# A hybrid encoder step: the second mixer's projections gathered ahead of its blocks, 13 unit pairs by seven products

## The chip, the cores and the metric

One core of a Trainium2 chip. The metric is the device time of one execution in microseconds (us), given as the median of several runs. TensorE is called PE in the rows of the profile (PEld where it loads weights), VectorE DVE, ScalarE ACT, GpSimd POOL; SP issues most of the DMAs.

## The reference

Two layers over 640 tokens (512 of a prompt, and 8 streams of 16): an FFN, a mixer and an FFN in each, each with a layer norm. The change lies in the second layer's mixer:

```python
proj = x @ w_in                       # 640 x 1024 by 1024 x (2048 gates z, 3072 xbc, 32 dt)
ext = concatenate([conv_state, xbc])  # three older rows ahead of each stream
xbc = silu(conv_b + sum(ext[:, w:w + length] * conv_w[w] for w in range(4)))
xs, bm, cm = ...                      # 4 groups of 8 heads; state of 128
dt = softplus(dt_raw + dt_bias)
y, h_last = ssd_recurrence(xs, dt, a, bm, cm, h0)   # chunk by chunk: causal part, then the carried state
yg = (y + d_skip * xs) * silu(z)
out = (yg * rsqrt(mean(square(yg)) + eps) * norm_g) @ w_out
```

## The kernel before

Every fp32 operand of the large matmuls is split into two fp32r parts, hi (a copy on ACT) and lo (the rest, a subtraction on DVE, line 101), and a product is hi·hi + hi·lo + lo·hi. x stands in SBUF as `xhi` and `xlo`, 8 blocks of 128 channels by 640 tokens. Weights come from memory into `raw` (four buffers of 128x1024) and are split into `w` (six buffers; `w1` holds one half-size unit).

A *unit* is 128 columns of an input projection. The plain way (`load_w`, `cm_proj`, `mm3`, line 146) takes it in two halves of 256 and 384 tokens, 24 matmuls each. The FFNs' gate and up projections work instead on *pairs* of units by seven products (`operands`, `matrix`, `product`, line 366): the weights of the pair and x are taken as 2x2 blocks, sums of blocks are formed (four of weights for each pair, on DVE, line 349; T1, T2, T4 and a fourth sum of x once), seven products of 12 matmuls over 320 tokens are made, and results are kept back on ACT (line 379) and added again.

The second mixer has 4 groups. A group has 6 xbc units (its B, C and four x units) and 4 gate units. `xbc` projects a unit into a row `ext` beside older rows, then convolves: the first step on ACT (1576), three taps on DVE (1578), Tanh on ACT (1580), two closing steps on DVE (1583, 1585); the result is stored in `bcx_d`. `gate_in` projects a gate unit and stores it in `z_d`. POOL fills `ext`'s older rows and copies the last rows out (1549 to 1570). A group is worked through in five *blocks* of 128 tokens: the streams (c = 4, `core_s`) first, then the prompt's four chunks in sequence (`core_b`); `core_a` prepares a block (loads of `bx`, `csb`, `ecs`; decays on DVE and ACT; small matmuls 1691 to 1701). `gate_out` gates a finished block, norms it and projects it out into `yacc` (24 matmuls of 512 columns, line 146 on `og`).

The order: four half units, dt and group 0's units come first; then 20 steps, one block each, with group g+1's xbc units and group g's gates as *fill* (`fill`, `run_fill`), up to two units a step. `gate_out` follows a group later. Within what buffers and dependencies allow, a scheduler places each engine's instructions, as the order below shows them.

Of the kernel before, what the change touches and what calls it, by code (L numbers as in the profile page):

```python
# [37 lines left out]
def kernel(ctx: ExitStack, tc: tile.TileContext, I, O, phases=PHASES):  # L38
# [186 lines left out]

    def ffn(i, ph, last, side=None):
# [3 lines left out]
        Q = T // 2  # L230
        with ExitStack() as st:
# [73 lines left out]
            hf32, lf32 = xh.bitcast(F32), xl.bitcast(F32)  # L305
            quad = lambda t, a, b: t[:, 4 * a:4 * a + 4, Q * b:Q * b + Q]

            tq = {n: wk.tile([128, 2, 4, Q], F32R, name=f"T{n}", bufs=1) for n in (1, 2, 4)}

            def both(t, p, m, op):  # L310

                u = wk.tile([128, T], F32, name="hf", bufs=2)[:, :Q]
                V.tensor_tensor(t, quad(hf32, *p)[:, k], quad(hf32, *m)[:, k], op=op)
                V.tensor_tensor(u, quad(lf32, *p)[:, k], quad(lf32, *m)[:, k], op=op)
                V.tensor_tensor(t, t, u, op=ALU.add)

            t2, t3 = (wk.tile([128, 4, Q], F32, name="h", bufs=4) for _ in range(2))
            for k in range(4):
                t1 = wk.tile([128, Q], F32, name="mx", bufs=2)
                both(t1, (0, 1), (1, 1), ALU.add)  # L320
                both(t3[:, k], (0, 0), (0, 1), ALU.subtract)
                for part in (hf32, lf32):
                    V.tensor_tensor(t2[:, k], t1 if part is hf32 else t2[:, k], quad(part, 0, 0)[:, k], op=ALU.subtract)
                split(tq[1][:, 0, k], tq[1][:, 1, k], t1)
                split(tq[2][:, 0, k], tq[2][:, 1, k], t2[:, k])

# [4 lines left out]
            for k in range(4):  # L331
                V.tensor_tensor(t2[:, k], quad(hf32, 1, 0)[:, k], t2[:, k], op=ALU.subtract)
                V.tensor_tensor(t2[:, k], t2[:, k], quad(lf32, 1, 0)[:, k], op=ALU.add)
                split(tq[4][:, 0, k], tq[4][:, 1, k], t2[:, k])
            X = {1: (quad(xh, 0, 0), quad(xl, 0, 0)), 2: (quad(xh, 1, 0), quad(xl, 1, 0)),
                 4: (quad(xh, 1, 1), quad(xl, 1, 1)), 3: (tq[4][:, 0], tq[4][:, 1]), 5: (tq[1][:, 0], tq[1][:, 1]),
                 6: (tq[2][:, 0], tq[2][:, 1]), 7: (quad(xh, 0, 1), quad(xl, 0, 1))}

            def operands(src0, src1):
                r0, r1 = raw_tile(), raw_tile()  # L340
                nc.sync.dma_start(r0, src0)
                nc.sync.dma_start(r1, src1)
                b11, b21, b12, b22 = r0[:, :512], r0[:, 512:], r1[:, :512], r1[:, 512:]
                u, v, w = (two_units() for _ in range(3))
                o = unit()

                def total(o, v, w):
                    with tc.issue_after(state["lo"]):
                        V.tensor_tensor(o, v, w, op=ALU.subtract)  # L349

                split2(u, r0)
                state["lo"] = split(v[:, 1, 0], v[:, 1, 1], b22).ins
                total(b11, b12, b11)
                split(v[:, 0, 0], v[:, 0, 1], b11)
                total(b12, b22, b12)
                total(b22, b22, b11)
                split2(w, r1)
                total(b21, b21, b22)
                split(o[:, 0], o[:, 1], b21)
                return {1: u[:, 0], 2: u[:, 1], 3: v[:, 1], 4: o, 5: v[:, 0], 6: w[:, 1], 7: w[:, 0]}  # L360

            def product(ps, A, p, first):
                n = 0
                for a, b in ((0, 0), (0, 1), (1, 0)):
                    for k in range(4):
                        nc.tensor.matmul(ps, A[p][:, a, k * 128:k * 128 + 128], X[p][b][:, k, :],  # L366
                                         start=(first and n == 0), stop=(n == 11), skip_group_check=True)
                        n += 1

            def matrix(A, take):  # L370

                z = sums[0]
                sums.reverse()
                x, w = (bank("a")[:, :Q] for _ in range(2))
                e = {}

                def keep(n, ps):
                    e[n] = wk.tile([128, Q], F32, name="mx", bufs=2)
                    nc.scalar.copy(e[n], ps)  # L379


                product(x, A, 1, True)
                nc.scalar.copy(z, x)  # L383
                product(w, A, 5, True)
                keep(5, w)
                product(z, A, 6, False)
                keep(2, z)
                product(x, A, 2, False)
                take(0, 0, x, None)
                product(z, A, 7, False)  # L390
                take(1, 1, z, e[5])
                product(w, A, 3, False)
                take(1, 0, w, e[2])
                product(z, A, 4, False)
                take(0, 1, z, None)
# [4 lines left out]
            def pair(f, before=None):  # L400
# [25 lines left out]
                for n, take in (("w_gate", gate), ("w_up", up)):  # L426
# [14 lines left out]
                    matrix(A, take)  # L441
# [1055 lines left out]
    def mixer1(ph, last):  # L1497
# [6 lines left out]
        with ExitStack() as st:  # L1504
            wk = pool("m1", 1, st, reuse_waits="tile")
            def after_norm():

                q = ExitStack()
                for n in ("pow", "ln"):
                    if n in state:  # L1510
                        q.enter_context(tc.issue_after(state[n]))
                return q

            with after_norm():
# [10 lines left out]
                cvo = {}  # L1525
# [12 lines left out]
            def row_tile(n):  # L1538
                return wk.tile([128, 667], F32, name=n, bufs=2)


            xin = {}

            def xbc_half(g, u, h):
                if h == 0:
                    m = (16 + g, 20 + g)[u] if u < 2 else 4 * g + u - 2
                    ext = row_tile("ext")
                    xin[g, u] = load_w(I["m1_in"][10 * g + u]), ext, m
                    G.memset(ext[:, 0:3], 0.0)
                    es_ = ext[:, 515:667].rearrange("p (b i) -> p b i", i=19)  # L1550
                    G.tensor_copy(es_[:, :, 0:3], cst[:, m].rearrange("p (b i) -> p b i", i=3))
                wt, ext, _ = xin[g, u]
                es_ = ext[:, 515:667].rearrange("p (b i) -> p b i", i=19)
                o, L = HALVES[h]
                ps = cm_proj(wt, h)
                if h == 0:
                    nc.scalar.copy(ext[:, 3:3 + L], ps[:, :L])
                else:
                    nc.scalar.copy(ext[:, 3 + o:515], ps[:, :512 - o])
                    nc.scalar.copy(es_[:, :, 3:19], ps[:, 512 - o:L].rearrange("p (b i) -> p b i", i=16))  # L1560

            def xbc(g, u):
                for h in range(0 if (g, u) not in xin else 1, 2):
                    xbc_half(g, u, h)
                _, ext, m = xin[g, u]
                es_ = ext[:, 515:667].rearrange("p (b i) -> p b i", i=19)
                if u == 0:
                    cvo[g] = wk.tile([128, 6, 27], F32, name="cvo", bufs=1)
                G.tensor_copy(cvo[g][:, u, 0:3], ext[:, 512:515])
                G.tensor_copy(cvo[g][:, u, 3:27].rearrange("p (b i) -> p b i", i=3), es_[:, :, 16:19])  # L1570
                if u == 5:
                    nc.sync.dma_start(O["conv"][:, 6 * g:6 * g + 6], cvo[g])
# [4 lines left out]
                for w in range(1, 4):  # L1577
                    V.scalar_tensor_tensor(acc[:, :n], ext[:, w:w + n], cw[:, m, w:w + 1], acc[:, :n],
                                           op0=ALU.mult, op1=ALU.add)
                nc.scalar.activation(ext[:, :n], acc[:, :n], AF.Tanh)  # L1580
                runs = lambda t: t[:, 515:667].rearrange("p (b i) -> p b i", i=19)[:, :, :16]
# [19 lines left out]
            def gate_in(g, q):  # L1601

                for h in range(0 if (g, q) not in zin else 1, 2):
                    gate_half(g, q, h)
                nc.sync.dma_start(z_d[g][:, :, q, :], zin[g, q][1].rearrange("p (c t) -> p c t", t=128))
# [7 lines left out]
            dt, cs = (wk.tile([32, T], F32, name=n) for n in ("dt", "cs"))  # L1613
            rst, te = (wk.tile([128, 1024], F32, name="csb", bufs=2)[:32, :T] for _ in range(2))
# [43 lines left out]
            def core_a(g, c):  # L1658
                bx = wk.tile([128, 6, 128], F32, name="bx", bufs=2)
# [4 lines left out]
                csb = wk.tile([128, 1024], F32, name="csb", bufs=2).rearrange("p (h t) -> p h t", t=128)  # L1664
# [6 lines left out]
                else:  # L1671
                    e8 = wk.tile([128, 8, 8], F32, name="e8")
# [4 lines left out]
                if 0 < c < 4:  # L1677
                    ecs = wk.tile([128, 4, 128], F32, name="ecs", bufs=1)
# [5 lines left out]
                elif c == 4:  # L1684
                    ecs = wk.tile([128, 8], F32, name="ecs8")
# [7 lines left out]
                cbm = wk.tile([128, 128], F32, name="cbm", bufs=2)  # L1693
# [3 lines left out]
                bk = wk.tile([128, 128], F32, name="bk", bufs=2)  # L1697
# [122 lines left out]
            for u in range(1, 6):  # L1820
                if u == 2:
                    gate_in(0, 0)
                    dt_rest()
# [196 lines left out]
```

## Time and profile before

| | |
|---|---|
| median of 3 runs | 2525.39 us (2525.12 to 2529.2) |
| the profiled execution | 2531.27 us, its span 2529.6 us |
| busy: TensorE, VectorE, ScalarE, GpSimd | 98%, 80%, 50%, 15% |
| second mixer in the span | about 1587 to 2084 us |

In a row of the instructions in order of time stand start, duration, engine, line, operation, output and inputs, shapes and count; in square brackets how long the engine had been idle and what ended that. A row of groups has the count, then the busy time, the mean in ns, and idle time before it. Rows of stretches give each engine's busy time between two moments. A matmul's duration includes its way through the pipeline; what one costs in a row of many is the distance of the starts.

### The profile page before, as it was taken

To read this page: it belongs to the slowest core of one execution; us is meant where nothing else is said; L and a number is where in the kernel's file an instruction comes from. 1 tells how busy PE (TensorE), PEld (TensorE's weight loads), DVE (VectorE), ACT (ScalarE), POOL (GpSimd) and SP (SyncE) were. 2 spreads that over 40 slices of the span, in tenths; PEclk is the share of its full clock that TensorE was granted. 3 is DMA by queue.
4 is the path that set the end of the run, shared out by engine and by line. 5 is a ranking of instruction groups with operands and counts; after the bars stand their busy time and mean duration, and the time that the engine had idled before them with its cause. 6 is when DMAs were issued, how large, how long until landed. Compare 5 with 4: busy or idle time off the path is not lost. (4 is left out here: it accounts for less than half of the span.)

```text
span 2529.6 us, 40802 instructions
## 1 busy us (share of the span) xinstructions
PE 2490.1 (98%) x15551; PEld 2286.1 (90%) x15551; DVE 2014.5 (80%) x3505; ACT 1269.2 (50%) x2389; POOL 373.5 (15%) x492
## 2 busy tenths in 40 slices
PE   9999999999999999999999999999999999999998
PEld 8999999878789999999999999998999879999897
DVE  7788777676879888877988887787575789998887
ACT  4444344336744555553555554566465543554542
POOL 0000001210130000013000002311121152111121
PEclk9999999999999999999999999999999999999999
DMA  5332335443222433452144434556464723555563
GB/s 186 109 100 78 116 112 161 144 150 117 87 79 64 119 102 97 112 164 66 59 114 113 120 100 132 158 162 204 137 211 137 242 74 99 154 151 165 151 172 116
DMA packets 179253, 324.80 MB, mean 128 GB/s; under 512 B 21312, under 2 KB 92608, under 8 KB 178544
## 3 DMA queue, kind: packets, MB, share of 16 engines
q1 hardware_dynamic: 165200, 293.83, 36.9%
q0 software_dynamic: 13856, 28.35, 5.8%
q8 instruction: 122, 2.00, 0.3%
q14 instruction: 75, 0.61, 0.1%
HBM read 259.56 MB, written 40.54 MB: 119 GB/s over the span
## 5 line engine op out<-in xcount | busy, mean ns | idle before, releaser
L100 ACT CAST w<-raw 128x512 fp32r<-128x512 f32 (+1 forms) x721 | 532.7, 769 | 337.3 <-DVE raw L349 144.7
L101 DVE TENSOR_TENSOR w<-raw,w 128x512 fp32r<-128x512 f32 (+2 forms) x721 | 621.2, 883 | 86.9 <-ACT w L100 84.0
L366 PE MATMUL bank<-xhi,w 128*128 128x320 f32 x2432 | 436.2, 309 | 2.3 <-DVE s L408 1.4
L366 PE MATMUL bank<-T,w 128*128 128x320 f32 x2736 | 428.2, 310 | 5.3 <-ACT bank L383 2.7
L366 PEld LDWEIGHTS bank<-T,w 128*128 128x128 f32 x2736 | 406.8, 188 | 8.6 <-ACT bank L383 5.3
L366 PEld LDWEIGHTS bank<-xhi,w 128*128 128x128 f32 x2432 | 376.8, 188 | 6.6 <-DVE s L408 2.2
L146 PE MATMUL bank<-xhi,w 128*128 128x256 f32 (+2 forms) x2272 | 364.3, 312 | 5.2 <-ACT xhi L100 2.6
L146 PEld LDWEIGHTS bank<-xhi,w 128*128 128x128 f32 x2272 | 337.3, 189 | 15.8 <-issue 4.9
L146 PE MATMUL bank<-w,h 128*128 128x512 f32 x1488 | 346.5, 391 | 0.2 <-DVE yacc L223 0.2
L146 PEld LDWEIGHTS bank<-w,h 128*128 128x128 f32 x1488 | 277.2, 188 | 57.9 <-ACT h L100 1.6
L366 PE MATMUL bank<-xlo,w 128*128 128x320 f32 x1216 | 227.8, 309 | 0.0
L349 DVE TENSOR_TENSOR raw<-raw 128x512 f32<-128x512 f32 x304 | 214.0, 704 | 3.4
L366 PEld LDWEIGHTS bank<-xlo,w 128*128 128x128 f32 x1216 | 190.8, 188 | 0.0
L146 PE MATMUL bank<-xlo,w 128*128 128x256 f32 (+2 forms) x1136 | 190.0, 309 | 0.0
L515 POOL DMA_DIRECT2D yacc<-ev x84 | 72.6, 893 | 690.2 <-ACT ev L514 619.8
L146 PEld LDWEIGHTS bank<-xlo,w 128*128 128x128 f32 x1136 | 171.6, 188 | 0.6
L502 PE MATMUL bank<-w,h 128*128 128x512 f32 x576 | 134.5, 390 | 0.0
L502 PEld LDWEIGHTS bank<-w,h 128*128 128x128 f32 x576 | 107.9, 188 | 22.7 <-DVE yacc L511 0.2
L379 ACT COPY mx<-bank 128x320 f32<-128x320 f32 x152 | 64.6, 425 | 105.9 <-PE bank L366 105.2
L223 DVE SCALAR_TENSOR_TENSOR yacc<-bank,yacc 128x512 f32<-128x512 f32 x120 | 82.0, 687 | 40.3 <-PE bank L146 39.7
L511 DVE SCALAR_TENSOR_TENSOR yacc<-bank,yacc 128x512 f32<-128x512 f32 x84 | 57.8, 688 | 67.4 <-PE bank L502 67.4
L146 PE MATMUL bank<-w,og 128*128 128x512 f32 x432 | 103.1, 394 | 0.0
(437 smaller groups left out, 3359.0 us busy)
## 6 DMA issues: line engine op xcount, KB each, us to landing
raw<-in_w_gate_dram SPq DMA_DIRECT2D x88, 512.0 KB, 3.7
raw<-in_w_up_dram SPq DMA_DIRECT2D x88, 512.0 KB, 3.8
raw<-in_w_down_dram SPq DMA_DIRECT2D x88, 512.0 KB, 3.6
raw<-in_m_in_dram SPq DMA_DIRECT2D x52, 512.0 KB, 4.6
yacc<-ev POOLq DMA_DIRECT2D x84, 256.0 KB, 4.7
raw<-in_m_out_dram SPq DMA_DIRECT2D x24, 512.0 KB, 4.3
csb<-cs_d SPq DMA_DIRECT2D x20, 512.0 KB, 5.3
h<-in_ssd_h_dram SPq DMA_DIRECT2D x16, 512.0 KB, 6.6
```

What stands on the lines that cost most here:

```text
L100: nc.scalar.copy(hi, src)
L101: return nc.vector.tensor_tensor(lo, src, hi.bitcast(F32), op=ALU.subtract)
L146: state["pe"] = nc.tensor.matmul(ps, a, b, start=(k == 0), stop=(k == n - 1)).ins
L223: state["acc"] = nc.vector.scalar_tensor_tensor(ya, pb, scale, ya, op0=ALU.mult, op1=ALU.add).ins
L349: V.tensor_tensor(o, v, w, op=ALU.subtract)
L366: nc.tensor.matmul(ps, A[p][:, a, k * 128:k * 128 + 128], X[p][b][:, k, :], start=(first and n == 0), stop=(n == 11), skip_group_check=True)
L379: nc.scalar.copy(e[n], ps)
L502: nc.tensor.matmul(ps, a[:, u], b[:, v], start=(first and n == 0), stop=(n == 5), skip_group_check=True)
L511: V.scalar_tensor_tensor(ya, ps, 0.5 / ALPHA, ya, op0=ALU.mult, op1=ALU.add)
L515: nc.gpsimd.dma_start(yacc[:, t, 512 * j:512 * j + 512], e, accum_op=ALU.add)
```

## The change

The FFNs keep their seven products; `x_sums`, `seven_x`, `operands` and `matrix` become functions that the second mixer calls too. The mixer falls into two parts. In the first, group 0's four gate units and dt are projected the plain way; then come the sums of x, and groups 0 to 2's xbc units and groups 1 and 2's gate units as 13 pairs by seven products. Group 3's first two xbc units follow the plain way. The second part has the 20 blocks, in which group 3's other four xbc units and its four gate units stand at steps 0, 1, 2, 3 and 6, 8, 10, 12. The first part's buffers (`m1a`: T1 to T4, three `ext`, four `acc`) are given up for the second's (`m1b`).

In the pairs the four sums of weights are made on POOL (line 270 of the changed kernel), as is one of the sums of x (lines 237 to 239). A convolved unit of a pair has two taps on DVE instead of three; the third is multiplied on ACT (`tap`, 1595) and added on POOL (1596).

```diff
+    def x_sums(tq, t2, t3, new_t1, new_u, E):
...
+        for k in range(4):
+            t1 = new_t1()
+            both(V, t1, (0, 1), (1, 1), ALU.add)
+            both(E, t3[:, k], (0, 0), (0, 1), ALU.subtract)
...
+    def operands(src0, src1, E=None):
...
+        def total(o, v, w):
+            with tc.issue_after(state["lo"]) if E is None else ExitStack():
+                (E or nc.vector).tensor_tensor(o, v, w, op=ALU.subtract)
+
+        split2(u, r0)
+        state["lo"] = split(v[:, 1, 0], v[:, 1, 1], b22).ins
+        total(b11, b12, b11)
+        split(v[:, 0, 0], v[:, 0, 1], b11)
+        total(b12, b22, b12)
+        total(b22, b22, b11)
+        split2(w, r1)
+        total(b21, b21, b22)
+        split(o[:, 0], o[:, 1], b21)
+        return {1: u[:, 0], 2: u[:, 1], 3: v[:, 1], 4: o, 5: v[:, 0], 6: w[:, 1], 7: w[:, 0]}
...
+            part = {"rows": wa, "ext": 3, "acc": 4}
...
-                for w in range(1, 4):
+                if two:
+                    tap = wa.tile([128, 667], F32, name="tap", bufs=1)
+                    nc.scalar.mul(tap[:, :n], ext[:, 1:1 + n], cw[:, m, 1:2])
+                    G.tensor_tensor(acc[:, :n], acc[:, :n], tap[:, :n], op=ALU.add)
+                for w in range(2 if two else 1, 4):
                     V.scalar_tensor_tensor(acc[:, :n], ext[:, w:w + n], cw[:, m, w:w + 1], acc[:, :n],
                                            op0=ALU.mult, op1=ALU.add)
...
+            def xbc_pair(g, u):
+                A = operands(I["m1_in"][10 * g + u], I["m1_in"][10 * g + u + 1], G)
+                es = [ext_tile(g, u + r) for r in range(2)]
...
+                        if e is None:
+                            nc.scalar.copy(o, v(ps))
+                        else:
+                            V.tensor_tensor(o, v(ps), v(e), op=ALU.add)
+                    if c != r:
+                        conv(g, u + r, ext, m, True)
+
+                matrix(X, sums, held, A, take)
+
+            def gate_pair(g, q):
+                A = operands(I["m1_in"][10 * g + 6 + q], I["m1_in"][10 * g + 7 + q], G)
...
+            x_sums(tq, t2, t3, held, lambda E: wa.tile([128, Q], F32, name="hf" if E is V else "hp", bufs=1), G)
+            for k in range(4):
+                split(tq[3][:, 0, k], tq[3][:, 1, k], t3[:, k])
+            X = seven_x(tq, tq[3][:, 0], tq[3][:, 1])
+            for g in range(3):
+                for u in (0, 2, 4):
+                    xbc_pair(g, u)
+                    if (g, u) == (0, 0):
+                        dt_rest()
+                for q in (0, 2):
+                    if g:
+                        gate_pair(g, q)
+            share("aaz", "bbbby")
+            xbc(3, 0)
+            xbc(3, 1)
+            first_part.close()
+            wb = part["rows"] = pool("m1b", 1, st, reuse_waits="tile")
...
-            fill = [(f, g + d, u) for g in range(4) for f, d, n in ((xbc, 1, 6), (gate_in, 0, 4)) for u in range(n)
-                    if g + d < 4 and (g + d, u) not in zin or f is xbc and g < 3]
...
+            fill = {i: (f, u) for i, (f, u) in zip((0, 1, 2, 3, 6, 8, 10, 12), [(xbc, u) for u in range(2, 6)] +
+                                                   [(gate_in, q) for q in range(4)])}
...
+                if i in fill:
+                    f, u = fill[i]
+                    f(3, u)
```

POOL in the mixer's first units, before: beside the mask work only the short memsets and copies of `ext` and `cvo`.

```order
L1569 COPY cvo<-ext 128x3
L1570 COPY cvo<-ext 128x24
L1549 MEMSET ext 128x3
L1551 COPY ext<-cst 128x8x3
L1569 COPY cvo<-ext 128x3
```

POOL there after the change: the last sums of x (`hp` holds a partial sum), the weight sums of the first two pairs (`raw`), and the first pair's convolutions with two sums of the third pair between them.

```order
L238 TENSOR_TENSOR hp<-xlo 128x320
L239 TENSOR_TENSOR w<-w,hp 128x320
L270 TENSOR_TENSOR raw<-raw 128x512 x8
L1584 COPY cvo<-ext 128x3
L1585 COPY cvo<-ext 128x24
L1596 TENSOR_TENSOR acc<-acc,tap 128x664
L1584 COPY cvo<-ext 128x3
L1585 COPY cvo<-ext 128x24
L270 TENSOR_TENSOR raw<-raw 128x512 x2
L1596 TENSOR_TENSOR acc<-acc,tap 128x664
```

Where short copies stood, weight sums of a later pair and convolution steps of an earlier one now alternate, each sum a full-width instruction with two inputs in SBUF.

DVE at a unit of the mixer before: split, taps, split, closing steps.

```order
L101 TENSOR_TENSOR w<-raw,w 128x512
L1578 SCALAR_TENSOR_TENSOR acc<-ext,cw,acc 128x664
L101 TENSOR_TENSOR w<-raw,w 128x512
L1578 SCALAR_TENSOR_TENSOR acc<-ext,cw,acc 128x664 x2
L1583 SCALAR_TENSOR_TENSOR cvs<-ext,acc 128x128
L1585 SCALAR_TENSOR_TENSOR acc<-ext,acc 128x512
```

DVE at a pair after the change (the third pair; `mx` are the results kept back, 1644 adds them).

```order
L1644 TENSOR_TENSOR ext<-bank,mx 128x320
L101 TENSOR_TENSOR w<-raw,w 128x512
L1598 SCALAR_TENSOR_TENSOR acc<-ext,cw,acc 128x664
L101 TENSOR_TENSOR w_16554<-raw,w_16554 128x512
L1598 SCALAR_TENSOR_TENSOR acc<-ext,cw,acc 128x664 x2
L1603 SCALAR_TENSOR_TENSOR cvs<-ext,acc 128x128
L1605 SCALAR_TENSOR_TENSOR acc<-ext,acc 128x512
L1598 SCALAR_TENSOR_TENSOR acc<-ext,cw,acc 128x664
L101 TENSOR_TENSOR w<-raw,w 128x2x512
L1603 SCALAR_TENSOR_TENSOR cvs<-ext,acc 128x128
L1605 SCALAR_TENSOR_TENSOR acc<-ext,acc 128x512
L101 TENSOR_TENSOR w<-raw,w 128x2x512
```

The splits of the next pair's weights are mixed with the convolution's taps, and the taps now wait for POOL's additions.

TensorE at the blocks of group 0, before: two projection units (256 and 384 columns) between one block's small matmuls and the next's.

```order
L1691 MATMUL bank<-bx 128x128
L1692 MATMUL bank<-ident,bx 128x128
L1701 MATMUL bank<-ident,bx 128x128 x4
L1727 MATMUL bank<-bx,hst 128x128 x4
L1731 MATMUL bank<-xe,bk 128x512
L1745 MATMUL bank<-csb,xd 64x128 x8
L146 MATMUL bank<-xhi,w 128x256 x16
L146 MATMUL bank<-xlo,w 128x256 x8
L146 MATMUL bank<-xhi,w 128x384 x16
L146 MATMUL bank<-xlo,w 128x384 x8
L146 MATMUL bank<-xhi,w 128x256 x16
```

TensorE there after the change.

```order
L1805 MATMUL bank<-csb,xd 64x128 x8
L1791 MATMUL bank<-xe,bk 128x512
L146 MATMUL bank<-w,og 128x512 x5
L1751 MATMUL bank<-bx 128x128
L1752 MATMUL bank<-ident,bx 128x128
L1761 MATMUL bank<-ident,bx 128x128 x4
L1787 MATMUL bank<-bx,hst 128x128 x4
L1805 MATMUL bank<-csb,xd 64x128 x8
L146 MATMUL bank<-w,og 128x512 x7
L1791 MATMUL bank<-xe,bk 128x512
```

The blocks follow each other with little between them, part of group 0's first output projection among it.

More of the change, by code (lines that the diff above doesn't have):

```diff
@@ L339, in operands @@
[L339 to L395, printed above, removed]
@@ L1827, in mixer1 @@
+            part["ext"] = part["acc"] = 2
+            ahead.extend(load_h0(wb, 0, j) for j in range(4))
             ORDER = (4, 0, 1, 2, 3)
             steps = [(g, c) for g in range(4) for c in ORDER]
[L1830 to L1836 removed]
```

242 lines of the change are left out of this document (147 added, 95 removed).

## Prediction

> **What bounds the kernel now.** I read the page's busy shares first, then busy time by stretches of the second mixer (from about 1587 to 2084 us of the span), then the instructions there in order of time.
>
> ```profile
> PE 2490.1 (98%) x15551; PEld 2286.1 (90%) x15551; DVE 2014.5 (80%) x3505; ACT 1269.2 (50%) x2389; POOL 373.5 (15%) x492
> ```
> ```profile
> core 0: us, PE busy (x) PEld busy (x) DVE busy (x) ACT busy (x) POOL busy (x), PEclk, DMA share, GB/s
> 1600.00:1650.00 50.00, 49.12 (x330) 46.76 (x329) 36.84 (x56) 29.67 (x56) 5.68 (x18) 1.00 0.59 182
> 1650.00:1757.00 107.00, 107.00 (x777) 101.57 (x776) 81.98 (x133) 74.06 (x206) 16.26 (x49) 1.00 0.59 178
> ...
> 2011.00:2051.00 40.00, 37.19 (x223) 28.77 (x222) 34.28 (x62) 20.16 (x52) 17.58 (x21) 1.00 0.43 134
> ```
>
> TensorE is the bound, in the mixer too: from 1650 to 1757 it never rests, DVE is busy for 77% and POOL for 15%. Only from 2011 on, where the blocks have no projection units left beside them, does TensorE miss 2.8 of 40 us. So fewer matmuls pay in full, as long as no other engine takes over. POOL looks idle; whether its time is free is the question.
>
> **Matmuls (gain).** 26 projection units in 13 pairs go from 48 matmuls a unit to 84 a pair. Here are the first row of one unit and of the next in the second mixer, and one row that comes once a pair in an FFN, which works by seven products already:
>
> ```profile
> 1633.69 1.98 PE L146 MATMUL bank<-xhi,w 128*128 128x256 f32 x16
> ...
> 1636.41 2.93 PE L146 MATMUL bank<-xhi,w 128*128 128x384 f32 x16
> ...
> 1640.57 1.98 PE L146 MATMUL bank<-xhi,w 128*128 128x256 f32 x16
> ```
> ```profile
> 1406.36 1.92 PE L366 MATMUL bank<-T,w 128*128 128x320 f32 x12
> ...
> 1418.66 1.92 PE L366 MATMUL bank<-T,w 128*128 128x320 f32 x12
> ```
>
> A unit takes 1640.57 - 1633.69 = 6.88 us (2.72 for its 256 columns, 4.16 for its 384), two take 13.76; a pair by products takes 12.30, or 1.76 a product. 13 x 1.46 = **19.0 us less**.
>
> **Sums on POOL (loss).** Each pair adds four 128x512 subtractions on POOL; each of the 18 convolved units adds one 128x664 addition there and takes one tap off DVE. What such work costs beside DVE is read where both have two SBUF inputs:
>
> ```profile
> 2066.95 1.29 POOL L193 TENSOR_TENSOR yacc<-yacc,h 128x512 f32<-128x512 f32 x1
> 2068.20 1.29 POOL L192 TENSOR_TENSOR yacc<-yacc,h 128x512 f32<-128x512 f32 x1
> ```
> ```profile
> 2143.65 1.04 POOL L1488 TENSOR_TENSOR h<-h,el 128x512 f32<-128x512 f32 x1 [35.21 <-DMA h<-in_ssd_h_dram]
> ```
> ```profile
> 2143.70 1.53 DVE L101 TENSOR_TENSOR w<-raw,w 128x512 fp32r<-128x512 f32 x1
> 2145.16 1.53 DVE L349 TENSOR_TENSOR raw<-raw 128x512 f32<-128x512 f32 x1
> 2146.61 0.68 DVE L223 SCALAR_TENSOR_TENSOR yacc<-bank,yacc 128x512 f32<-128x512 f32 x1
> ```
> ```profile
> 2102.82 0.49 DVE L313 TENSOR_TENSOR mx<-xhi 128x320 f32<-128x320 f32 x1
> 2103.22 0.49 DVE L313 TENSOR_TENSOR h<-xhi 128x320 f32<-128x320 f32 x1
> ```
> ```profile
> 2103.44 3.99 POOL L1488 TENSOR_TENSOR h<-h,el 128x512 f32<-128x512 f32 x1 [7.90 <-DMA h<-in_ssd_h_dram]
> ```
>
> The split at 2143.70 takes 1.53 us and ends at 2145.23, 0.54 after POOL's instruction ended (2144.69): it stood still until then. The one behind it suffers the same from POOL's next; L223, with one input in PSUM, does not. The other way round POOL's instruction at 2103.44 needs 3.99 us for 1.04 of work, as long as DVE runs from SBUF without a break. So on two SBUF inputs the two engines take turns, and their times add. Prices from start to start:
>
> ```profile
> 1639.25 0.69 DVE L101 TENSOR_TENSOR w<-raw,w 128x512 fp32r<-128x512 f32 x1
> 1639.85 0.91 DVE L1578 SCALAR_TENSOR_TENSOR acc<-ext,cw,acc 128x664 f32<-128x664 f32 x1
> 1640.67 0.69 DVE L101 TENSOR_TENSOR w<-raw,w 128x512 fp32r<-128x512 f32 x1
> ...
> 1643.09 0.29 DVE L1583 SCALAR_TENSOR_TENSOR cvs<-ext,acc 128x128 f32<-128x128 f32 x1 [0.91 <-ACT ext L1580]
> 1643.30 0.68 DVE L1585 SCALAR_TENSOR_TENSOR acc<-ext,acc 128x512 f32<-128x512 f32 x1
> ```
> ```profile
> L101 DVE TENSOR_TENSOR w<-raw,w 128x1024 fp32r<-128x1024 f32 x248 | 301.0, 1227 | 31.5 <-ACT w L100 30.9
> ```
>
> A split of 512 is 0.60, a tap 0.82, the two last steps of a unit 0.21 and 0.60; a split of 1024 is 1.23, or 1.14 with the same 0.09 of overlap. While TensorE works on one pair, DVE and POOL finish the convolutions of the pair before and prepare the weights of the next:
>
> - DVE: splits 2 x 1.14 + 3 x 0.60 = 4.08; two convolutions of 2 x 0.82 + 0.81 = 4.90; together 8.98.
> - POOL: 4 x 1.25 = 5.00 (2068.20 - 2066.95), and 2 x 1.25 x 664/512 = 3.24; together 8.24.
>
> In turns that is 17.2 us against 12.30 of TensorE; with 0.54 for a 512 split where the other engine's end hides the start-up, 16.3. I take 16.8, 4.5 over. It binds in nine periods: while pairs 2 to 7 and 10 to 12 run (groups 1 and 2 have three convolved pairs, then two gate pairs). In the others the splits and sums, 9.1, or these and a gate's two short DVE steps, stay under 12.30. 9 x 4.5 = **40.5 us more**; between 25 (POOL gets ahead in gate periods, so only the whole stretch counts) and 58 (another 1.5 us a period in which both wait for ACT or TensorE; the convolution goes ACT, POOL, DVE, ACT, DVE, and DVE has the next pair's splits queued behind its taps).
>
> ACT's share of a period is hidden by this, though not by much:
>
> ```profile
> L1576 ACT ACTIVATE acc<-ext,cw 128x664 f32<-128x664 f32 x24 | 22.8, 951 | 0.0
> ```
> ```profile
> L100 ACT CAST w<-raw 128x512 fp32r<-128x512 f32 (+1 forms) x721 | 532.7, 769 | 337.3 <-DVE raw L349 144.7
> ...
> L379 ACT COPY mx<-bank 128x320 f32<-128x320 f32 x152 | 64.6, 425 | 105.9 <-PE bank L366 105.2
> ```
>
> Five casts at a mean of 0.77 (3.9), six passes over 664 (first step, new tap and Tanh of two units) at no more than 0.95 (5.7), three 320-column copies of kept products at 0.43 (1.3) and about as much again into the rows make 12.2: under 16.8, and about level with TensorE's 12.30. So if DVE and POOL did not bind, ACT would be next, with nothing to spare.
>
> [...]
>
> **The start.** The sums of x come before the first pair.
>
> ```profile
> 1599.37 1.03 PE L209 MATMUL bank<-ident,yacc 128*128 128x128 f32 x8
> ...
> 1604.91 2.96 PE L146 MATMUL bank<-xhi,w 128*32 128x384 f32 x16
> ...
> 1609.11 2.94 PE L146 MATMUL bank<-xhi,w 128*128 128x384 f32 x16
> ```
> ```profile
> 1602.27 1.27 DVE L211 TENSOR_TENSOR xlo<-bank,xhi 128x512 fp32r<-128x512 f32 x2
> ```
>
> After the last transposes (1600.4) TensorE has 2.72 + 4 x 4.16 + 4.20 (the dt half, 1609.11 - 1604.91) = 23.6 us of plain work, to 1624.0. x is whole at 1603.5. Then DVE has 44 instructions of 320 columns at 0.40 (2103.22 - 2102.82), 17.6, and POOL 12 at 1.25 x 320/512 = 0.78, 9.4; in turns to 1630.5, and the order puts the first pair's first split behind them: 1631.6, 7.6 us late. The third product waits for three sums more, about 2 us. **10 us**; 0 if the engines overlapped (1603.5 + 17.6 + 1.1 is before 1624), 14 if the clock falls.
>
> **The blocks.** Eight units instead of 31 stand between the 20 blocks: 12 steps have none, where three had.
>
> ```profile
> 2020.69 0.46 PE L1691 MATMUL bank<-bx 128*128 128x128 f32 x2 [0.67 <-DMA bx<-bcx_d]
> ...
> 2031.82 0.49 PE L1691 MATMUL bank<-bx 128*128 128x128 f32 x2 [0.39 <-DMA bx<-bcx_d]
> ...
> 2035.82 0.43 PE L1745 MATMUL bank<-csb,xd 128*64 128x128 f32 x2 [1.04 <-DVE xd L1705]
> 2036.95 0.38 PE L1799 MATMUL bank<-ones,zz 128*128 128x2 f32 x2 [0.70 <-POOL zz L1798]
> ```
> ```profile
> 1759.58 0.77 PE L1691 MATMUL bank<-bx 128*128 128x128 f32 x2 [2.50 <-DMA bx<-bcx_d]
> ...
> 1768.24 2.80 PE L146 MATMUL bank<-xhi,w 128*128 128x256 f32 x16
> ```
> ```profile
> 1986.64 0.38 PE L1691 MATMUL bank<-bx 128*128 128x128 f32 x2
> ...
> 1991.11 2.08 PE L146 MATMUL bank<-xhi,w 128*128 128x256 f32 x16
> ```
>
> The three steps without units lost 2.80 us, 0.93 each; nine more make 8.4. The wait of 2.50 goes, since these loads then have stood ready for long, and with it the slow clock behind it: the same matmuls took 8.66 us there and 4.47 later, so 6.7 in all. Group 0's blocks have six convolutions and no output projection beside them; 3 us more (0 to 10, DVE being 86% busy in the nearest stretch). **5 us more**, between -5 and 15. The second part's buffers lie where the sums of x lay, so the blocks' first loads wait for the last gate pair; in the order TensorE has five units after it, 5 x 6.88 = 34 us, ahead of the first block's matmuls, which covers these loads and the first block's steps on ACT and DVE. On SP's queue the weights come in the same order ahead of the stores, and the blocks read rows stored long before: nothing.
>
> **Sum:** -19.0 + 40.5 + 10 + 5 = +36.5. The profiled execution is 2531.27 us (span 2529.6), 5.9 above the median of 2525.39; on the median, **2562 us**. 0.2% (5 us) is about what a measurement tells from no change.
>
> **Rivals.**
>
> - *POOL's sums run beside DVE.* Then DVE's 8.98 stay under 12.30, the start waits for nothing, and -19.0 + 5 gives 2511. For it: POOL has 85% of its time. Against: the rows at 2143 to 2146. It decides if a 512 split stays at 0.69 beside POOL's sums. 14%.
> - *Sums fit into gaps.* They take turns, but where DVE waits for a product anyway: 20 + 5 - 5 - 19 is about 2526. Against: DVE alone needs 9 of 12.3. 6%.
> - *The clock falls.* If each period's 4.5 us comes as one wait, two products at half pace follow, 3.5 a period: 2593. For it: 2.50 us sufficed at 1759. Against: a pair waits in pieces, at the products whose weights are late. 12%. [...]
>
> The forecast itself has 68%; the ends of its terms give 2526 (25, 0, -5) to 2593 (58, 14, 15). 8 times in 10 the time lies within 2518 to 2606: above the first rival; the third lies inside, with some of the way that the upper ends would add to it. Faster 0.14, same 0.06, slower 0.80.
>
> **What would show it.** Pairs about 17 us apart in the nine periods and 12.3 in the gate periods; splits and taps with means well over 0.70 and 0.91 beside POOL's sums; TensorE waiting for L101's splits of w; a wait of 7 to 8 us before the first product; blocks without units about 10 us apart. Wrong if pairs come every 12.3 us.

## The result, and the profile after

The changed kernel takes 2635.59 us (median of 5 runs, 2631.99 to 2643.24) against 2527.08 us of the kernel before in the same series: a ratio of 1.0432, 95% interval 1.0413 to 1.0451, or 108.5 us more. The forecast was 2562, the range 2518 to 2606. The profiled execution took 2643.24 us (span 2641.5), 112 more than the one shown of before. One execution of a later variant (three `bx` buffers) took 4407.7 us at a granted clock of 0.744 and is left out of that variant's figures.

The page after: TensorE does fewer matmuls and is busy for longer, and its granted clock sinks in the slices of the second mixer.

```profile
PE 2513.6 (95%) x15395; PEld 2292.9 (87%) x15395; DVE 2094.1 (79%) x3579; ACT 1319.6 (50%) x2448; POOL 498.7 (19%) x574
...
PEclk9999999999999999999999999899979899999999
```

Outside the mixer the two traces differ by 4 us in all, in favour of the changed kernel. The mixer in four stretches (busy time of each engine, then the clock): the 13 pairs, five plain units, the first seven steps of the blocks (group 0's five and the first two in which group 1 begins), and the rest up to the first transposes behind the mixer (the output projection's last two chunks of 128 tokens come after them).

```profile
1622.05:1852.67 230.62, 186.06 (x1109) 178.72 (x1109) 172.47 (x220) 128.25 (x220) 130.33 (x140) 0.90 0.36 107
1852.67:1886.29 33.62, 33.52 (x237) 33.20 (x235) 20.45 (x30) 14.94 (x31) 2.47 (x14) 1.00 0.65 202
1886.29:1974.90 88.61, 60.18 (x348) 46.73 (x349) 52.60 (x88) 56.33 (x174) 14.85 (x19) 0.81 0.56 169
1974.90:2183.20 208.30, 184.59 (x1036) 147.46 (x1035) 149.79 (x267) 114.37 (x307) 57.10 (x72) 0.93 0.54 169
```

The pairs take 230.6 us where 13 x 12.30 = 159.9 would be plain work: **70.7 too much**. In the blocks TensorE stands still for 28.4 + 23.7 = 52.1 us, and the trace's records of the granted clock put 65 of their 297 us at half pace (0.50). An estimated 44 of these fell on work, which costs another 22 (TensorE's busy time in them, which includes the way through the pipeline, is 50, which would be 25). Before, the same two losses around the blocks were 6 and 5 us. So the blocks lose 74 - 11 = **63 us**, as an estimate. With the 19.0 that the matmuls give: 70.7 + 63 - 19 = 115; the mixer grew by 112 + 4 = 116.

What TensorE waited for, in the pairs and then in the blocks: total, times, longest.

```profile
PE bank L289 <- ACT bank L303: 25.6, 10, 3.3
PE bank L289 <- DVE w L101: 5.4, 1, 5.4
PE bank L289 <- DVE ext L1644: 5.3, 6, 2.4
```
```profile
PE bank L1751 <- DMA bx<-bcx_d: 23.3, 8, 8.6
PE bank L1859 <- POOL zz L1858: 12.8, 6, 4.3
PE bank L146 <- ACT og L100: 5.0, 2, 4.4
```

One period of the pairs, in order of time:

```profile
1704.16 1.52 DVE L101 TENSOR_TENSOR w<-raw,w 128x512 fp32r<-128x512 f32 x1
...
1707.55 2.66 POOL L270 TENSOR_TENSOR raw<-raw 128x512 f32<-128x512 f32 x2
...
1707.92 1.93 PE L289 MATMUL bank<-T,w 128*128 128x320 f32 x12
...
1710.17 1.58 POOL L1596 TENSOR_TENSOR acc<-acc,tap 128x664 f32<-128x664 f32 x1
...
1711.79 0.85 ACT L1595 ACTIVATE tap<-ext,cw 128x664 f32<-128x664 f32 x1 [2.26 <-POOL acc L1596]
1711.79 0.94 DVE L1598 SCALAR_TENSOR_TENSOR acc<-ext,cw,acc 128x664 f32<-128x664 f32 x1 [4.26 <-POOL acc L1596]
1712.54 0.42 ACT L303 COPY bank<-bank 128x320 f32<-128x320 f32 x1
...
1713.01 3.05 PE L289 MATMUL bank<-T,w 128*128 128x320 f32 x12 [3.17 <-ACT bank L303]
1713.26 3.08 DVE L1598 SCALAR_TENSOR_TENSOR acc<-ext,cw,acc 128x664 f32<-128x664 f32 x2
```

POOL's two weight sums hold up its addition for the convolution (1710.17); ACT's second tap waits for that addition, since there is one `tap` buffer; the copy of a product (L303) stands behind this tap on ACT; and TensorE's next product waits 3.17 us for the copy and then runs at half pace for a while (3.05 us for twelve matmuls instead of 1.93). At the same time the two engines slow each other: a split takes 1.52 us instead of 0.69, two taps 3.08 instead of 1.7. So two theories for the pairs: **A, turns** (the forecast's: two-input work on DVE and POOL adds up) and **B, chain** (ACT and TensorE wait for POOL's late result). For the blocks: **C**, they are slow by themselves, and **D**, the forecast's, they are not.

### The profile page after: what moved, and what is told of

It is laid out like the page before. It is cut to its first block, busy times and chain, and to the rows that moved or that the text cites. A ratio compares the mean times of both kernels' runs of the same rounds, so it can differ in the third digit from the quotient of the medians.

```text
span 2641.5 us, 40781 instructions
## 1 busy us (share of the span) xinstructions
PE 2513.6 (95%) x15395; PEld 2292.9 (87%) x15395; DVE 2094.1 (79%) x3579; ACT 1319.6 (50%) x2448; POOL 498.7 (19%) x574
## 5 line engine op out<-in xcount | busy, mean ns | idle before, releaser
L101 DVE TENSOR_TENSOR w<-raw,w 128x512 fp32r<-128x512 f32 (+2 forms) x734 | 658.9, 919 | 87.6 <-ACT w L100 84.9
L289 PE MATMUL bank<-T,w 128*128 128x320 f32 x3360 | 538.5, 314 | 32.2 <-ACT bank L303 27.4
L289 PEld LDWEIGHTS bank<-T,w 128*128 128x128 f32 x3360 | 509.5, 191 | 39.6 <-ACT bank L303 33.5
L289 PE MATMUL bank<-xhi,w 128*128 128x320 f32 x2744 | 499.6, 311 | 16.8 <-DVE w L101 5.4
L289 PEld LDWEIGHTS bank<-xhi,w 128*128 128x128 f32 x2744 | 429.9, 190 | 24.1 <-DVE ext L1644 7.5
L146 PE MATMUL bank<-xhi,w 128*128 128x384 f32 (+4 forms) x1440 | 231.1, 311 | 6.5 <-DVE yacc L1870 3.3
L146 PEld LDWEIGHTS bank<-xhi,w 128*128 128x128 f32 (+1 forms) x1440 | 213.1, 187 | 11.6 <-DVE yacc L1870 4.3
L289 PEld LDWEIGHTS bank<-xlo,w 128*128 128x128 f32 x1372 | 218.0, 190 | 0.0
L300 ACT COPY mx<-bank 128x320 f32<-128x320 f32 x178 | 75.1, 424 | 112.0 <-PE bank L289 111.5
L146 PE MATMUL bank<-xlo,w 128*128 128x256 f32 (+3 forms) x720 | 119.9, 307 | 0.0
L223 DVE SCALAR_TENSOR_TENSOR yacc<-bank,yacc 128x512 f32<-128x512 f32 x120 | 81.9, 686 | 39.5 <-PE bank L146 38.9
L146 PEld LDWEIGHTS bank<-w,og 128*128 128x128 f32 x432 | 87.0, 205 | 25.7 <-ACT og L100 5.9
```

Source lines behind the costliest of these rows:

```text
L101: return nc.vector.tensor_tensor(lo, src, hi.bitcast(F32), op=ALU.subtract)
L146: state["pe"] = nc.tensor.matmul(ps, a, b, start=(k == 0), stop=(k == n - 1)).ins
L223: state["acc"] = nc.vector.scalar_tensor_tensor(ya, pb, scale, ya, op0=ALU.mult, op1=ALU.add).ins
```

## The experiments

**Two tap buffers.** The cheapest cut of chain B.

```diff
-                    tap = wa.tile([128, 667], F32, name="tap", bufs=1)
+                    tap = wa.tile([128, 667], F32, name="tap", bufs=2)
```

> The changed kernel as it is (2636 us), but with two buffers for `tap` instead of one. In the changed kernel a pair with convolutions takes 17.8 us, and TensorE waits 3.2 us in it for a copy on ACT (L303). Theory A (turns, the prediction's): DVE's 9.0 and POOL's 8.2 us of two-input work add up and set the period; a buffer changes neither, so 2636 within 5 us, and the period stays 17.8. Theory B (chain): ACT cannot start the second unit's tap before POOL has read the first one, and POOL's addition stands behind two sums of weights; the copy that TensorE needs stands behind that tap on ACT. With two buffers the copy comes about 2.3 us earlier, TensorE's wait falls below 1 us and the half clock behind it goes: some 2.3 + 1.7 us in each of 9 periods, so 2590 to 2610, unless DVE, which waits 4.3 us a period for POOL's addition with a split of w behind it, becomes the next wait (then 2615 to 2630).

2632.1 us, ratio to before 1.0418 (1.0403 to 1.0434); the pairs take 230.4 us, as long as with one buffer. The waits only change their name:

```profile
PE bank L289 <- ACT mx L300: 24.0, 8, 3.9
PE bank L289 <- ACT bank L303: 6.6, 7, 1.6
```

The 25.6 us behind L303 became 24.0 behind L300. The wait that the chain shows was where the delay came out, not what made it. B falls in this form. It is not excluded in another: DVE itself waits for POOL's additions in the changed kernel's pairs, and with two `tap` buffers it still does, for 39.1 us.

```profile
DVE acc L1598 <- POOL acc L1596: 38.9, 10, 5.5
```

**POOL's work moved back to DVE**, piece by piece: the sums of weights (`operands(..., G)` without `G`), the third tap (`conv(..., True)` without `True`), and both.

> The changed kernel, but the four sums of weights of a pair are made on DVE (as in the FFNs) instead of POOL; the third tap stays on ACT and POOL. Theory A (turns): DVE 9.0 + 4 x 0.6 = 11.4, POOL 3.2: 14.6 a period instead of 17.2, 2.6 x 9 = 23 us less: 2613. Theory B (chain): POOL's addition no longer stands behind two sums (2.6 us), so ACT's second tap and the copy behind it come 2.4 us earlier and the half clock goes with the wait: about 4 us x 9 less, 2595 to 2605. This run alone does not tell the two apart; with the one that has two tap buffers it does.

> The changed kernel, but a convolved unit of a pair has three taps on DVE again (no tap on ACT, no addition on POOL); the sums of weights stay on POOL. Theory A (turns): DVE 9.0 + 2 x 0.82 = 10.6, POOL 5.0, in turns 15.6 instead of 17.2: 1.6 x 9 = 14 us less, 2622, and TensorE waits for L101's splits. Theory B (chain): ACT waits for POOL nowhere, TensorE's copy comes in time, the period falls to 13 to 14 us: 4 to 5 us x 9 less and no half clock, 2590 to 2600. In both the blocks (297 us from the first block to the end of the output projection) are as long as in the changed kernel.

> The changed kernel with both moved back to DVE in the pairs: sums of weights and the third tap; POOL keeps only its sum of x ahead of the pairs. DVE then has 9.0 + 2.4 + 1.6 = 13.0 us a period, TensorE 12.3. Both theories: a period of 13.0 to 13.5, so 4.3 to 4.8 us x 9 and no half clock behind the waits: 2580 to 2595. If it comes out above 2610, neither the turns nor the chain is what holds the pairs. The blocks stay as in the changed kernel, so that the kernel stays some 55 us slower than before (2527) whatever the pairs do.

Measured: 2612.7 (ratio 1.0337, 1.0322 to 1.0352), 2623.4 (1.0383, 1.0367 to 1.0398) and 2596.0 (1.0271, 1.0251 to 1.0290). A had said 2613, 2622 and 2580 to 2595, and is met to 1.5 us. The blocks stayed at 288 to 293 us in all three. B had asked for 2595 to 2605 in the first, and for 2590 to 2600 with the taps back on DVE, where no `tap` on ACT waits for POOL any more; they came out at least 7 and 23 us above that. The third does not tell A from B. Nor does the pair stage follow DVE's wait for POOL's additions: the wait is 38.9 us in the changed kernel's 230.6, 11.8 in 203.4 with the sums on DVE, and none in 218.5 with the taps on DVE.

**Idle POOL work.** To part turns from waiting for results for good: the kernel without POOL's work, and on top of it POOL work whose result nobody reads. The work stands ahead of each pair's products. The first of two kernels subtracts; the second has `G.tensor_copy(dm, v(0))` in the last line.

```diff
+            def idle_pool(A):
+                for p in (1, 2, 7, 6):
+                    dm = wa.tile([128, 512], F32, name="dm", bufs=1)
+                    v = lambda a: A[p][:, a].bitcast(F32)
+                    G.tensor_tensor(dm, v(0), v(1), op=ALU.subtract)
```

> The kernel with POOL's work back on DVE (2596 us, its pairs 188 us), and on top of it four subtractions of 128x512 for each pair on POOL, of the two halves of split weights into a scratch tile that nobody reads: as much two-input work as the sums of weights were, but no engine waits for its result. Turns on the SBUF inputs: DVE's 13.0 us a period grow by 4 x 1.25 less what of it falls into DVE's pauses, 3 to 4.5 in nine periods and less than 1 in the others: 2596 + 27 to 43, 2623 to 2640, with DVE's splits and taps longer than 0.70 and 0.91. If what cost time was only that others waited for POOL's results: 2596 within 4.

> The same, but POOL's four idle instructions are copies of 128x512 (one SBUF input) instead of subtractions. If the two engines take turns only where both have two SBUF inputs: 2596 within 4, DVE's splits at 0.70. If any POOL work on SBUF holds DVE up: 2596 plus some 20 to 35 us.

The subtractions cost 44 us: 2640.3 (1.0440, 1.0423 to 1.0458), at the upper end of what turns give, with a pair stage as long as the changed kernel's (232.9 and 230.6 us) although nothing reads the subtractions' results. DVE hardly waits here; it is busy for 223.6 of the 232.9 us, and its own instructions take longer. Groups of DVE's instructions between 1625 and 1805 us (count, busy time, mean), first without POOL's work, then with the idle subtractions:

```profile
L1598 DVE SCALAR_TENSOR_TENSOR acc<-ext,cw,acc 128x664 f32<-128x664 f32 x54 | 47.0, 901 | 0.7 <-ACT acc L1592 0.7
...
L101 DVE TENSOR_TENSOR w<-raw,w 128x512 fp32r<-128x512 f32 x42 | 28.3, 682 | 0.0
```
```profile
L1598 DVE SCALAR_TENSOR_TENSOR acc<-ext,cw,acc 128x664 f32<-128x664 f32 x42 | 41.8, 1026 | 1.1 <-ACT acc L1592 1.1
...
L101 DVE TENSOR_TENSOR w<-raw,w 128x512 fp32r<-128x512 f32 x32 | 35.2, 1103 | 0.0
```

A split grows from 682 to 1103 ns, a tap from 901 to 1026. The copies cost 12 us (2608.0; 1.0320, 1.0304 to 1.0335), neither of the two values expected (2596, or 20 to 35 us more): one-input work on POOL holds DVE up as well, less.

```profile
L101 DVE TENSOR_TENSOR w<-raw,w 128x512 fp32r<-128x512 f32 x36 | 29.0, 809 | 0.0
```

A split takes 809 ns here, against 682 without POOL's work. That does not agree with the forecast's reading, two inputs on both sides: a copy has one.

The pair stages of four of these kernels (stretch, its length, TensorE's busy time, and so on), in this order: sums on DVE, taps on DVE, both, both with idle subtractions.

```profile
1622.08:1825.47 203.39, 172.89 (x1110) 165.24 (x1110) 183.00 (x271) 127.03 (x220) 84.16 (x88) 0.97 0.40 122
```
```profile
1621.89:1840.39 218.50, 184.82 (x1110) 178.85 (x1110) 189.98 (x237) 114.92 (x202) 119.31 (x122) 0.90 0.38 113
```
```profile
1622.79:1810.62 187.83, 171.17 (x1110) 166.79 (x1110) 178.92 (x286) 114.13 (x200) 43.81 (x70) 0.95 0.42 127
```
```profile
1623.87:1856.77 232.90, 187.22 (x1110) 177.25 (x1110) 223.61 (x285) 112.81 (x197) 126.93 (x122) 0.91 0.34 101
```

Beside the forecast's sums for a period (DVE + POOL in turns):

| kernel | DVE + POOL, us a period | pair stage, us |
|---|---|---|
| both on DVE | 13.0 + 0 | 187.8 |
| sums on DVE | 11.4 + 3.2 = 14.6 | 203.4 |
| taps on DVE | 10.6 + 5.0 = 15.6 | 218.5 |
| changed kernel | 9.0 + 8.2 = 17.2 | 230.6 |
| both on DVE, idle subtractions | 13.0 + 5.0 = 18.0 | 232.9 |

The stage has nine such periods, and from the first row to the changed kernel each microsecond of the sum costs about ten in it: (230.6 - 187.8) / (17.2 - 13.0) = 10.2. From row to row this varies, from 3 to 15, so the sum gives the order and the rough size, no more. Idle work costs about as much as work that is waited for. What the changed kernel's waits for POOL's results add to the turns was not measured apart. Copies do not add in full: at 0.6 us each (a cast of 128x512 on POOL took 0.61 in the kernel before), four of them would make the sum 15.4 and the stage some 212 us, and it takes 198.9.

**Blocks alone.** The two parts, but nothing by products.

```diff
-            for g in range(3):
-                for u in (0, 2, 4):
-                    xbc_pair(g, u)
...
+            for g in range(3):
+                for u in range(6):
+                    xbc(g, u)
+                for q in range(4):
+                    if g:
+                        gate_in(g, q)
```

> The changed kernel's two parts, but the units of the first part by the plain way (48 matmuls a unit): no products, no sums of x or of weights, no POOL in the convolutions. The blocks and their 8 units are untouched. Theory C (the blocks are slow by themselves, since most of the units that stood between them are gone): from the first block to the end of the output projection 285 to 297 us as in the changed kernel, and the whole is what the changed kernel is without its pairs' loss, 2636 - (71 - 19) = 2584. Theory D (the prediction's: the blocks lose 5 us, and what is lost beyond comes from the pairs, from POOL or the slow clock that they leave behind): blocks near 235 us, the whole at 2532.

2590.6 us, ratio 1.0251 (1.0234 to 1.0269), 66 us slower than before with every matmul of before. The blocks take nearly as long as in the changed kernel (288 and 297 us), in the same two stretches:

```profile
1843.31:1929.97 86.66, 61.90 (x381) 48.13 (x382) 56.27 (x96) 60.28 (x193) 14.17 (x20) 0.84 0.58 176
1929.97:2131.20 201.23, 177.51 (x1003) 141.82 (x1002) 145.10 (x258) 110.55 (x291) 56.65 (x72) 0.94 0.55 172
```

C holds, D falls: gathering the units ahead of the blocks costs some 65 us by itself; the forecast's upper end for the blocks was 15.

**Why a block is slow alone.** Rows of the changed kernel in two uncovered steps (SPq is the issue of a load):

```profile
1925.37 0.50 SPq L1720 DMA_DIRECT2D bx<-bcx_d  x1
...
1929.79 0.46 PE L1751 MATMUL bank<-bx 128*128 128x128 f32 x2 [1.44 <-DMA bx<-bcx_d]
...
1934.31 1.14 DVE L1812 SCALAR_TENSOR_TENSOR yb<-bx,chp,yb 128x128 f32<-128x128 f32 x4
...
1935.47 0.33 SPq L1720 DMA_DIRECT2D bx<-bcx_d  x1
...
1941.17 0.77 PE L1751 MATMUL bank<-bx 128*128 128x128 f32 x2 [6.78 <-DMA bx<-bcx_d]
...
1947.04 1.14 DVE L1812 SCALAR_TENSOR_TENSOR yb<-bx,chp,yb 128x128 f32<-128x128 f32 x4
...
1949.73 0.83 SPq L1720 DMA_DIRECT2D bx<-bcx_d  x1
...
1956.77 0.79 PE L1751 MATMUL bank<-bx 128*128 128x128 f32 x2 [8.57 <-DMA bx<-bcx_d]
```

It is a ring: DVE's last reading of a `bx` (L1812) ends at 1935.45, the load into that buffer is issued at 1935.47 and lands at 1941.17, and only then does TensorE go on, since it meets the next block's `bx` ahead of this block's own matmuls; these let DVE finish at 1948.2, and the next load is issued at 1949.73. 11.4 and 15.6 us, whatever the engines have to do.

```diff
-                bx = wb.tile([128, 6, 128], F32, name="bx", bufs=2)
+                bx = wb.tile([128, 6, 128], F32, name="bx", bufs=3)
...
-                    ecs = wb.tile([128, 4, 128], F32, name="ecs", bufs=1)
+                    ecs = wb.tile([128, 4, 128], F32, name="ecs", bufs=2)
```

> The changed kernel with three buffers instead of two for a block's loaded rows `bx`, and two instead of one for `ecs` (whose load stands ahead of the next `bx` on SP's queue). Theory E (a ring): TensorE meets the next block's `bx` ahead of this block's own matmuls; `bx` is loaded only when the block before has read its buffer to the end (L1812), and lands 4.5 to 7 us later; so load, matmuls and DVE's closing steps follow each other in a ring of 11 to 16 us whatever the engines have to do. With a third buffer the load starts a block earlier: the 23 us of waits for `bx` go, and most of the half clock behind them: 2595 to 2610. Theory F (DVE's and ACT's own steps, the store of a gate unit and `zz` on SP's queue set the pace): another wait takes its place, 2625 to 2636.

2612.7 us (2612.4 to 2619.5), ratio 1.0352 (1.0331 to 1.0373): 20 to 23 us less than the changed kernel, by the ratios and by the medians, just short of what E gave (26 to 41) and more than F did. The blocks take 269.2 us instead of 297, and the waits for `bx` fall from 23.3 to 9.0:

```profile
PE bank L1859 <- POOL zz L1858: 10.0, 7, 2.7
PE bank L1751 <- DMA bx<-bcx_d: 9.0, 4, 6.0
```

So the ring is part of it; `bx` and `ecs` were not tried apart. The other waits (for the sum of squares `zz` and for DVE's and ACT's steps, F) stay.

**More cover.** Group 2's units not as pairs, but between the blocks: 18 units there instead of 8.

```diff
-            for g in range(3):
+            for g in range(2):
...
-            xbc(3, 0)
-            xbc(3, 1)
+            xbc(2, 0)
+            xbc(2, 1)
...
+            fill = dict(enumerate([(xbc, 2, u) for u in range(2, 6)] +
+                                  [v for k in range(4) for v in ((xbc, 3, k), (gate_in, 2, k))] +
+                                  [(xbc, 3, 4), (xbc, 3, 5)] + [(gate_in, 3, q) for q in range(4)]))
```

> The changed kernel, but group 2's units are no pairs: two xbc units stand plain ahead of the blocks, and the other eight, with group 3's ten, one at each of the steps 0 to 17. So 8 pairs by products instead of 13, and 18 units instead of 8 between the blocks. Without any effect on the blocks: five pairs fewer lose 7.3 us of matmuls and give back the 17 us by which these five exceeded 12.3 us each: 2626. Theory C (cover): the blocks' 52 us of waits and 22 us of half clock lie in some 14 uncovered steps, 4 to 5 us each; ten more are covered, so 40 to 50 us less: 2575 to 2590.

2588.3 us, ratio 1.0246 (1.0230 to 1.0262), within what cover gives (2575 to 2590). The blocks:

```profile
1806.29:2126.67 320.38, 298.20 (x1862) 253.62 (x1862) 236.70 (x412) 197.16 (x539) 80.85 (x115) 0.97 0.58 183
```

They are 23.5 us longer with ten more units, which are 68.8 us of matmuls: 45 us less is lost, 30 of it in waits (320.4 - 298.2 = 22.2 instead of 52.1), the rest by the clock (0.97 in this row, 0.81 and 0.93 in the changed kernel's).

**Everything that helped**, and then two gate units of group 1 ahead of the sums of x (7 pairs):

> All that helped or may help, together: weight sums and third tap on DVE, three `bx` and two `ecs`, group 2's units between the blocks (8 pairs). From 2596 with POOL's work back on DVE: 12 to 18 us less for the blocks' cover beyond what the third buffer gives, 30 for the buffer, 3 to 5 for the pairs: 2540 to 2560 if cover and ring are the two sides of one wait, and not below before (2527), since the first pair still comes some 12 us late after the sums of x and only 8 x 1.46 = 11.7 us of matmuls are saved.

> The version with everything that helped (2559 us), and two gate units of group 1 plain ahead of the sums of x (so 7 pairs). TensorE then has 13.8 us more of plain work while DVE and POOL make the sums of x, of which their own splits and closing steps cost DVE about 4.5: the first pair comes some 9 us less late, one pair fewer costs 1.5: 2559 - 7.5 = 2551. If the first pairs are late for another reason (the weights of the second pair, which ACT and DVE split after the sums), 2557 to 2562.

2559.4 (1.0135, 1.0119 to 1.0151) and 2553.9 us (1.0106, 1.0091 to 1.0121); expected were 2540 to 2560, and 2551 or else 2557 to 2562. With the two units TensorE no longer waits for the first pair's splits of w, 5.3 us in the version without them; what it waits for in the pairs of the second version is

```profile
PE bank L289 <- ACT w L100: 3.7, 1, 3.7
PE bank L289 <- DVE acc L1619: 3.5, 1, 3.5
PE bank L289 <- ACT bank L303: 3.3, 2, 2.8
```

No version beats the kernel before. A pair saves 1.46 us of matmuls, and a unit taken from between the blocks cost 2.9 us on average (66 us for 23 units). What makes up the last 26 us was not broken down further.

**The third `bx` in the kernel before**, with three `h0` buffers instead of four to make room.

> The kernel before (its interleaved order, nothing by products in the mixer), with three `bx` and two `ecs`; to make room, three buffers instead of four for `h0`, the carried states that a streams' block reads (the fourth is loaded when the first is free). With the units between its blocks TensorE there waits only 2.50 us for `bx` once, with 4.7 us of half clock behind it, and 0.4 to 0.7 us each in the three last steps. Ring: these go, 7 to 9 us less, 2517 to 2520; the fourth state, which comes later, may give up to 5 of it back. Cover (the units hide what the ring costs, so that the buffer is worth nothing there): 2522 to 2530.

2536.6 us, ratio 1.0041 (1.0026 to 1.0055): 0.4% slower, where both theories had asked for 2530 at most. No wait for `bx` is left in its trace, and the slow clock behind it is gone (from 1757 to 1800 us the granted clock is 1.00, in the kernel before 0.88); the carried states come late instead:

```profile
PE bank L1769 <- DMA h<-in_ssd_h_dram: 2.9, 3, 2.2
PE bank L1799 <- POOL zz L1798: 2.1, 2, 1.1
```

These rows explain a few microseconds, not all of the 11 by which the medians differ (the profiled execution, 2533 us, is among its quickest). The edits were not tried apart; what the third buffer alone is worth there stays open.

## Why the prediction was wrong

The direction was right and the size far too small. By its steps:

- **Matmuls, -19.0**: right. A pair without disturbance takes 12.3 to 12.4 us (the thirteenth), and the plain matmuls are those counted.
- **The sums on POOL, +40.5 (25 to 58)**: the turns are right, the size is too small. From the start of one pair's first product to the next one's, the nine periods take 55.4 us more than 9 x 12.30, 6.2 each instead of 4.5. The turns themselves hold (the table, and the idle subtractions). Added to them is what the forecast had as a rival, the clock: the pairs have 44 us at half pace, which cost TensorE an estimated 17.5, some of it in the first pair.

```profile
1677.35 2.03 PE L289 MATMUL bank<-T,w 128*128 128x320 f32 x12 [2.03 <-ACT bank L303]
...
1730.85 3.49 PE L289 MATMUL bank<-T,w 128*128 128x320 f32 x12 [2.59 <-ACT bank L303]
```

  A wait of 2.03 us left the clock as it was (2.03 us for twelve), one of 2.59 did not (3.49). The forecast gave the clock 12%, on its estimate that a pair waits in pieces; the second row is one wait, and the trace has the clock at half from 1730.72 on. Yet no length of a wait decides by itself. In the blocks of the same trace 22 matmuls that came 1.6 us after a wait of 1.91 us (at 2042.29) took 6.43 us, where 22 without one (at 2052.01) took 5.28. In the pairs 24 that came 1.5 us after a wait of 1.77 us (at 1651.83) took 5.22 instead of 3.68. That TensorE would wait for L101's splits in the periods was wrong: it waits for ACT's copies, and the run with two tap buffers shows that this name is interchangeable. The forecast also left out that DVE would stand still for POOL's additions (38.9 us).
- **The start, +10 (0 to 14)**: the size is right, 12.3 us over in the first pair, in part by luck. The forecast wait of 7 to 8 us before the first product is one of 5.36 us inside it, after eight of its twelve matmuls; smaller waits and half pace (the next product took 3.57 us) make up the rest.

```profile
1628.74 1.44 PE L289 MATMUL bank<-xhi,w 128*128 128x320 f32 x4 [5.36 <-DVE w L101]
```

- **The gate periods, 0**: 3.1 us in all; nearly right.
- **The blocks, +5 (-5 to 15)**: this is the step that failed; it is +63, and 66 measured by itself. Its size came from three steps without units at the end of the kernel before, 0.93 us of waiting each, taken for nine more. Such steps, a prompt chunk behind another with a whole output projection of 24 matmuls (5.7 us) beside it, still cost 0.5 to 1.7 us in the changed kernel. But the steps that became uncovered were mostly of other kinds. The first seven, group 0's above all, have one output projection among them: 28.4 us of waits (the third stretch above) and an estimated 9 by the clock, where the forecast had put 3. The steps into and out of the streams' blocks of groups 2 and 3, which load four carried states and store their split inputs, lose some 29 more (an estimate of waits and clock, step by step from TensorE's rows); the forecast gave them no price of their own. The 6.7 us of a wait that was to vanish did not matter beside this.
- **SP's queue and the passage between the parts, nothing**: the passage is covered, as said (33.6 us for five units). SP's queue does stand at stores and single buffers, with loads behind them: in the blocks 30.9 us in three waits at the store of a gate unit (L1628) and 30.1 us in seven at the load into the one `ecs` (L1740). That is one side of the ring.

The sum at the terms' measured sizes, -19.0 + 55.4 + 12.3 + 3.1 + 63, is +115, less 4 outside the mixer, against 112 between the two profiled executions. The upper end of the blocks' term rested on the same three rows and on at most 10 us for group 0, so the range could not reach this.

## What to carry to other kernels

Work that stands between two dependent steps is worth what it hides as well as what it costs: before it is gathered elsewhere, each kind of step must be priced without it (load, transposes, closing steps and the buffer's return in a ring), not the one kind that happened to be bare already. Work moved from VectorE to GpSimd was not off the path here, where both had two inputs in SBUF (subtractions that nobody reads cost 44 us): start from the sum of the two engines' times. And a wait's name is no proof; two buffers at the place that the chain names, here, only moved the name.

## What the runs showed of the hardware that was not expected

- GpSimd work that nobody waits for cost 44 us on top of 2596, and one-input copies still 12 (splits of 682 ns became 1103 and 809).
- The clock fell at single waits of 2.6 us in the changed kernel, and 0.7 us after one of 1.91, but not after one of 2.03. In the pairs half pace came in pieces of 3.4 or 6.8 us, in the blocks up to 13.7, so a period with one piece of 3.4 paid up to 1.7 us more, half of it (an estimate). All pieces of the mixer in that trace begin on one grid of 3.41 us (the last, at 2116.43, 143 steps after the first, at 1628.33); how a wait lies to it may decide, which was not tested.
